# Attention's product with V: one fp32 operand in two column halves of the array in place of a split operand in whole-array matmuls

## The chip, the cores and the metric

The kernel runs on one core of a Trainium2 chip. A core has a matrix engine (TensorE, with a loader for its stationary operand), VectorE, ScalarE, GpSimd, and queues that issue DMAs. Each engine executes its own instructions in order and waits for the others through semaphores. The metric is the device time of one execution in microseconds; lower is better.

## What is computed

Two layers of a hybrid block run on 1024 latent tokens and 256 context tokens of width 1024. Each layer has a projection into four groups of heads (a state-space mixer, a gated recurrence, global attention, windowed attention), an output projection and an MLP. The change is in the attention of groups C (global) and D (windowed). Cut to that, the reference is:

```python
def block(qblk):                       # group C, 128 queries at a time
    s = einsum('bqhgd,bkhd->bhgqk', qblk, k_all) * scale
    pr = softmax(s, axis=-1)
    return einsum('bhgqk,bkhd->bqhgd', pr, v_all)

# group D: 128 queries see three blocks of 128 keys around them, the context, and a sink logit
pr = softmax(concatenate([s_band, s_ctx, s_sink], axis=-1), axis=-1)
o = (einsum('bnhgqk,bnkhd->bnqhgd', pr[..., :nk], vw)
     + einsum('bnhgqk,bkhd->bnqhgd', pr[..., nk:nk + n_ctx], vc))
```

There are four query heads of width 64 in each group and two key heads, so two query heads share a key head. Everything is fp32.

## The kernel before, in words

The kernel keeps fp32 accuracy with the faster matmul type fp32r by splitting operands: a high part rounded to fp32r and a low part, the remainder. `mm3` (lines 141 to 143) takes a product as three matmuls of such parts; most of the kernel's matmuls are these, in the projections.

Attention is done in units of one key head and its two query heads. `unit_proj` makes a unit's queries, keys and values for ten tiles of 128 tokens, and `unit_post` finishes two tiles at a time. It writes V as a tile of 128 columns per key block: columns 0 to 63 hold the fp32r high part (a ScalarE copy), columns 64 to 127 the low part (VectorE's subtraction, line 572).

`attention` walks over query tiles. For each, `attn_head` or `attn_both` makes the scores in PSUM, VectorE takes the maximum (L648), ScalarE the exponential. `attn_av` then multiplies the probabilities by V. Its `turn` takes two key blocks: TensorE transposes four 128x128 pieces (two blocks, two heads, L718) into one PSUM tile `pt`; ScalarE copies that tile as fp32r into `th` (recorded under its helper's line, L130); VectorE subtracts it from the original into the low part `tl` (L722). `prod`, run one turn later, adds two matmuls for each key block into the PSUM tile `po`: V's two parts times `th` (L727) and times `tl` (L728), each 128 columns stationary by 256 moving, fp32r. So po's partitions 0 to 63 hold the high part's product and 64 to 127 the low part's; at the end ScalarE copies the lower half (`lo`), VectorE adds the two (L744) and scales by the reciprocal sums (L746), which TensorE has spread out by two transposes (L741).

A global tile has ten key blocks, a windowed one five (four at the two ends of the sequence), a context tile two. Over both layers that makes 488 products of a query tile and a key block. Two `pt` tiles, three `qk` tiles and one `po` tile rotate in PSUM, and eight tiles tagged `s` in SBUF serve `th`, `tl` and others.

Attention is not run alone. `weave` interleaves its steps with those of another stage's projections, and the framework's scheduler puts the resulting instructions of each engine into one order, by its own costs. That order is fixed when the kernel is built, so a change of instructions also moves their neighbours. The modulation product (L319, in `mod_bank`) is the one place that already uses column tiles: fp32, 32 columns stationary, 512 moving, at four column positions.

Of the kernel before, what the change touches and what calls it, by code (L numbers as in the profile page):

```python
# [8 lines left out]
F32R = mybir.dt.float32r  # L9
# [4 lines left out]
P = 128  # L14
# [26 lines left out]
def f(ap):  # L41
    return ap.bitcast(F32)
# [51 lines left out]
class Net:  # L94
# [390 lines left out]
    def unit_proj(self, l, h, ws, rope_r, with_dt, need_ctx):  # L485

        nc = self.nc
        hh, hl = h
        nw = WU if with_dt else 256
        ws = [[t.rearrange("p (k c) -> p k c", k=4) for t in w] for w in ws]  # L490
        q = self.U()[:, :].rearrange("p (c d) -> p c d", d=P)
        kT = self.U(F32R)
        V = self.U(F32R).rearrange("p (c d) -> p c d", d=P)
        if with_dt:
            self.dtr = self.tp.tile([P, NT, 8], F32, tag="dtr", name="dtr", bufs=1)
        g = self.L[l]["rw"][:, rope_r:rope_r + 128]
        posts, half = [], None
        for tp in range(NT // 2):
            qkv = self.B()
            n1 = self.B()  # L500
            qkv3 = qkv.rearrange("p (a c) -> p a c", a=2)
            ps2 = self.PS() if not with_dt else None
            kv_only = tp == 0 and not with_dt and not need_ctx
            if kv_only:

                for k in range(KD):
                    wh, wl = (t[:, k % 4, P:256] for t in ws[k // 4])
                    self.mm3(ps2[:, 0:256], wh, wl, hh.at(k, 0, 256), hl.at(k, 0, 256), k == 0, k == KD - 1)
                    if k % 4 == 3:
                        yield 1.3  # L510
                self.copy_a(n1[:, 0:256], ps2[:, 0:256])
                for a in range(2):
                    nc.tensor.transpose(ps2[:, 256 + a * P:256 + a * P + P], n1[:, a * P:a * P + P], self.ident)
                last = self.copy_a(qkv3[:, :, P:256], ps2[:, 256:512].rearrange("p (a c) -> p a c", a=2))
            for a in range(0 if kv_only else 2):
                tt = 2 * tp + a
                t0 = tt * P
                if (0 if t0 < CTX else CTX + (t0 - CTX) // 512 * 512) not in hh.done:
                    yield from hh.pending
                ps = self.PS()[:, :nw] if with_dt else ps2[:, a * 256:a * 256 + 256]  # L520
                for k in range(KD):
                    wh, wl = ws[k // 4]
                    self.mm3(ps, hh.at(k, t0, P), hl.at(k, t0, P), wh[:, k % 4, :nw], wl[:, k % 4, :nw], k == 0, k == KD - 1)
                    if k % 4 == 3:
                        yield 1.3
                if with_dt:
                    last = self.copy_a(qkv3[:, a, :], ps[:, 0:256])
                    self.copy_a(self.dtr[:, tt, :], ps[:, 256:264])
            if not with_dt and not kv_only:
                last = self.copy_a(qkv, ps2)  # L530
            if half:
                with self.tc.issue_after(last.ins):
                    posts.append(half())
            if len(posts) == 2:
                posts.pop(0)()
                yield 0.3
            half = self.unit_post(tp, qkv3, n1[:, 0:384], q, kT, V, g, kv_only)
        self.tails = posts
        self.half = half
        return q, kT, V  # L540

# [8 lines left out]

    def unit_post(self, tp, qkv3, n1, q, kT, V, g, kv_only):
        nc = self.nc

        q0 = 2 if kv_only else 0
        nh = 3 - q0
        qk = qkv3[:, :, 64 * q0:192]
        v = qkv3[:, :, 192:256]
        vs = V[:, 2 * tp:2 * tp + 2, :]
        n1v = n1.rearrange("p (a c) -> p a c", a=2)
        n14 = n1.rearrange("p (a g d) -> p a g d", a=2, d=64)  # L560
        self.act(n1v[:, :, 64 * q0:192], qk, AF.Square)
        ss = self.tiny(2 * nh)
        ss3 = ss.rearrange("p (a g) -> p a g", a=2)
        nc.vector.tensor_reduce(ss3, n14[:, :, q0:3], axis=AX.X, op=ALU.add)

        if not kv_only:
            nc.vector.tensor_scalar(ss3[:, :, 0:2], ss3[:, :, 0:2], 64.0 * EPS, None, op0=ALU.add)
        nc.vector.tensor_scalar(ss3[:, :, nh - 1:nh], ss3[:, :, nh - 1:nh], 1.0 / 64.0, EPS, op0=ALU.mult, op1=ALU.add)
        rs = self.tiny(2 * nh)
        nc.gpsimd.tensor_tensor(rs, ss, self.mhalf.to_broadcast([P, 2 * nh]), op=ALU.pow)  # L570
        self.copy_a(vs[:, :, 0:64], v)
        nc.vector.tensor_sub(vs[:, :, 64:128], v, f(vs[:, :, 0:64]))
        def half():
            nc.vector.tensor_mul(n14[:, :, q0:3], qk.rearrange("p a (g d) -> p a g d", d=64),
                                 rs.rearrange("p (a g) -> p a g", a=2)[:, :, :, None].to_broadcast([P, 2, nh, 64]))
            qd = q[:, 2 * tp:2 * tp + 2, :]
            ks = n14[:, :, 2]
            gq = g[:, None, None, 0:64].to_broadcast([P, 2, 2, 64])
            gk = g[:, None, 64:128].to_broadcast([P, 2, 64])
            q4 = qd.rearrange("p a (g d) -> p a g d", g=2)  # L580
            nc.vector.tensor_mul(ks, ks, gk)
            if tp == 0 and not kv_only:
                nc.vector.tensor_mul(q4, n14[:, :, 0:2], gq)
            if tp:
                nc.vector.tensor_mul(n14[:, :, 0:2], n14[:, :, 0:2], gq)
                n3 = qkv3[:, :, 0:192]
                n1x, n3x = (t.rearrange("p a (g x h e) -> p a g x h e", g=3, x=2, h=2) for t in (n1v, n3))

                rc = slice(2 * tp - 2, 2 * tp), slice(8, 9)
                bc = [P, 2, 3, 16]  # L590
                for x in range(2):
                    for hf in range(2):
                        nc.vector.tensor_mul(n3x[:, :, :, x, hf], n1x[:, :, :, x, 1 - hf],
                                             self.sin[:, rc[x], None, hf].to_broadcast(bc))
                for x in range(2):
                    for hf in range(2):
                        nc.vector.tensor_mul(n1x[:, :, :, x, hf], n1x[:, :, :, x, hf],
                                             self.cos[:, rc[x], None].to_broadcast(bc))
                nc.vector.tensor_add(qd, n1v[:, :, 0:128], n3[:, :, 0:128])
                nc.vector.tensor_add(ks, ks, n3[:, :, 128:192])  # L600

            st = qkv3.rearrange("p a (s d) -> p a s d", d=64)[:, :, 0:2]
            self.copy_a(st[:, :, 0].bitcast(F32R), ks)
            nc.vector.tensor_sub(st[:, :, 1], ks, st[:, :, 0])

            def post():
                pt = self.PS("qk")
                for a in range(2):
                    nc.tensor.transpose(pt[:, a * P:a * P + P], st[:, a].rearrange("p s d -> p (s d)"), self.ident)
                self.copy_a(kT[:, 2 * tp * P:2 * tp * P + 256], pt[:, 0:256])  # L610
            return post
        return half
# [92 lines left out]

    def attn_av(self, prs, V, keys, mix):

        nc = self.nc
        kcs = [(k0 // P) + j for (k0, n) in keys for j in range(n // P)]
        po = self.PS("po")  # L710

        def turn(i):
            two = kcs[i:i + 2]
            w = 256 * len(two)
            pt = self.PS("pt")
            for e in range(len(two)):
                for hd in range(2):
                    nc.tensor.transpose(pt[:, e * 256 + hd * P:e * 256 + hd * P + P],  # L718
                                        prs[hd][0][:, (i + e) * P:(i + e) * P + P], self.ident)
            th, tl = self.S(w, F32R), self.S(w, F32R)  # L720
            self.copy_a(th, pt[:, :w])
            nc.vector.tensor_sub(tl, pt[:, :w], f(th))  # L722

            def prod():
                for e, kc in enumerate(two):
                    c = slice(e * 256, e * 256 + 256)
                    nc.tensor.matmul(po[:, :256], V[:, kc, :], th[:, c], start=i + e == 0, stop=False)  # L727
                    nc.tensor.matmul(po[:, :256], V[:, kc, :], tl[:, c], start=False, stop=i + e == len(kcs) - 1)  # L728
            return prod
        prod = None  # L730
        for i in range(0, len(kcs), 2):
# [901 lines left out]
```

## Time and profile before

| what | value |
|---|---|
| median of three runs | 3107.41 us (3104.35 to 3108.75) |
| profiled execution | 3102.39 us |
| its span, first to last instruction | 3100.6 us |
| TensorE busy | 2972.3 us, 96% |
| VectorE busy | 2195.9 us, 71% |
| ScalarE busy | 1516.4 us, 49% |
| GpSimd busy | 800.6 us, 26% |
| mean granted TensorE clock | 0.988 of full speed |

A busy time is the union of an engine's instructions. Matmuls are pipelined: a record runs on into its successors, so the step from one start to the next tells what a matmul costs in a stream, and the recorded duration does not. PE is TensorE, PEld its weight loader, DVE VectorE, ACT ScalarE, POOL GpSimd. L722 is line 722 of the kernel; the changed kernel's lines are shifted by one to two behind the edits.

### The profile page before, as it was taken

The numbers are of one execution on the slowest core, as the hardware profiler recorded it, in microseconds if no ns is written. First come the engines' busy times: TensorE is split into PE (matmuls) and PEld (weight loads), VectorE is DVE, ScalarE is ACT, GpSimd is POOL, SyncE is SP. The second block draws the span as 40 slices with busy tenths as digits, with TensorE's granted clock in tenths as the row PEclk, the third lists the DMA queues.
The fourth block names the chain that finished last, engine by engine and source line by source line (L and its number), as shares of the span: only waits on it lengthen the run. The fifth ranks groups of instructions, "written<-read, shape, count | busy, mean of one in ns | idle before, by whom it ended". The sixth has DMA issues, their size and how long they took to land.

```text
span 3100.6 us, 45540 instructions
## 1 busy us (share of the span) xinstructions
PE 2972.3 (96%) x16210; PEld 2458.7 (79%) x16210; DVE 2195.9 (71%) x4385; ACT 1516.4 (49%) x3570; POOL 800.6 (26%) x708
## 2 busy tenths in 40 slices
PE   5998998989999999999999999999899999999999
PEld 2788887788889887788888688887788778778887
DVE  5778777787742656577777777778787886667775
ACT  4675776676544444321112577676675544442120
POOL 2214123241454100222111512223342510032220
PEclk9999998999999999999999999999999999999999
DMA  8200012330355545642222400112422564553231
GB/s 283 64 18 25 20 37 72 98 138 33 125 168 157 177 152 182 218 146 85 77 84 78 147 18 18 28 40 70 140 82 71 171 205 138 166 179 104 87 104 62
DMA packets 241076, 330.71 MB, mean 107 GB/s; under 512 B 37328, under 2 KB 159824, under 8 KB 240848
## 3 DMA queue, kind: packets, MB, share of 16 engines
q1 hardware_dynamic: 213200, 281.64, 28.5%
q10 hardware_dynamic: 27648, 46.15, 4.0%
q8 instruction: 128, 2.10, 0.3%
q14 instruction: 100, 0.82, 0.1%
HBM read 253.28 MB, written 74.45 MB: 106 GB/s over the span
## 4 chain that ended last, share of the span: by engine, by line
PE 58%; DVE 5%; ACT 4%; DMA 2%; POOL 2%; issue 2%; ACTq 0%; SPq 0%; POOLq 0%; DVEq 0%
PE qk L143 8%; PE qk L142 8%; PE qk L141 8%; PE pm L143 6%; PE pm L141 6%; PE pm L142 6%; PE pt L142 3%; PE pt L143 3%; PE pt L141 3%; PE pt L718 1%; DVE u L136 1%; PE po L727 1%; POOL wl L246 1%; PE po L728 1%; DMA u<-in_w_ffn 1%
## 5 line engine op out<-in xcount | busy, mean ns | idle before, releaser
L246 POOL TENSOR_TENSOR wl<-raw,wh 128x512 fp32r<-128x512 f32 (+1 forms) x224 | 318.8, 1437 | 1215.9 <-ACT wh L130 916.5
L141 PE MATMUL pm<-u,wh 128*128 128x512 f32 (+1 forms) x1271 | 473.8, 373 | 4.1 <-DVE u L136 2.8
L143 PE MATMUL pm<-u,wl 128*128 128x512 f32 (+1 forms) x1271 | 467.5, 368 | 1.3 <-POOL wl L246 1.3
L142 PE MATMUL pm<-u,wh 128*128 128x512 f32 (+1 forms) x1271 | 466.5, 367 | 0.0
L130 ACT ACTIVATE wh<-raw 128x512 fp32r<-128x512 f32 (+1 forms) x224 | 135.6, 628 | 484.2 <-PE qk L142 159.8
L143 PE MATMUL qk<-u,wl 128*128 128x512 f32 (+1 forms) x874 | 326.7, 374 | 1.0 <-POOL wl L246 1.0
L141 PE MATMUL qk<-u,wh 128*128 128x512 f32 (+1 forms) x874 | 324.5, 372 | 1.9 <-DVE b L1342 1.0
L130 ACT ACTIVATE s<-pt 128x512 fp32r<-128x512 f32 (+4 forms) x548 | 251.2, 467 | 120.2 <-PE pt L718 74.4
L142 PE MATMUL qk<-u,wh 128*128 128x512 f32 (+1 forms) x810 | 300.2, 371 | 2.2 <-POOL u L409 1.8
L136 DVE SCALAR_TENSOR_TENSOR u<-pm,mods,u 128x512 f32<-128x512 f32 (+1 forms) x313 | 216.5, 693 | 90.4 <-PE pm L143 89.2
L141 PEld LDWEIGHTS pm<-u,wh 128*128 128x128 f32 x1271 | 243.1, 191 | 41.2 <-DVE u L136 4.4
L143 PEld LDWEIGHTS pm<-u,wl 128*128 128x128 f32 x1271 | 242.6, 191 | 35.4 <-POOL wl L246 2.7
L142 PEld LDWEIGHTS pm<-u,wh 128*128 128x128 f32 x1271 | 243.1, 191 | 30.8
L136 DVE SCALAR_TENSOR_TENSOR u<-qk,mods,u 128x512 f32<-128x512 f32 (+1 forms) x294 | 203.7, 693 | 84.2 <-PE qk L143 83.4
L133 ACT ACTIVATE b<-b 128x512 f32<-128x512 f32 (+4 forms) x256 | 146.1, 571 | 154.6 <-DVE b L1346 123.4
L133 ACT ACTIVATE e<-qk,t 128x512 f32<-128x512 f32 (+2 forms) x336 | 188.3, 571 | 42.3 <-DVE t L651 27.2
L722 DVE TENSOR_TENSOR s<-pt,s 128x512 fp32r<-128x512 f32 (+1 forms) x256 | 166.8, 661 | 39.7 <-ACT s L130 37.2
L1394 DVE TENSOR_TENSOR u<-e,u 128x256 fp32r<-128x256 f32 (+1 forms) x160 | 160.3, 1019 | 48.8 <-ACT u L130 27.6
L141 PEld LDWEIGHTS qk<-u,wh 128*128 128x128 f32 x874 | 165.2, 189 | 34.3 <-ACT u L130 1.7
L143 PEld LDWEIGHTS qk<-u,wl 128*128 128x128 f32 x874 | 164.6, 188 | 31.7 <-POOL wl L246 1.8
L141 PE MATMUL pm<-wh,u 128*128 128x256 f32 (+1 forms) x592 | 177.8, 301 | 3.3 <-ACT b L133 1.7
L142 PEld LDWEIGHTS qk<-u,wh 128*128 128x128 f32 x810 | 152.9, 189 | 31.3 <-POOL u L409 2.7
(325 smaller groups left out, 7526.3 us busy)
## 6 DMA issues: line engine op xcount, KB each, us to landing
raw<-in_w_ffn SPq DMA_DIRECT2D x184, 256.0 KB, 2.9
e<-in_w_mod SPq DMA_DIRECT2D x64, 512.0 KB, 4.5
u<-in_w_ffn SPq DMA_DIRECT2D x60, 512.0 KB, 5.1
m<-b ACTq DMA_DIRECT2D x96, 256.0 KB, 2.0
e<-m SPq DMA_DIRECT2D x32, 640.0 KB, 4.3
u<-in_w_mod SPq DMA_DIRECT2D x32, 512.0 KB, 6.3
e<-m SPq DMA_DIRECT2D x32, 512.0 KB, 3.9
raw<-in_w_in SPq DMA_DIRECT2D x48, 256.0 KB, 2.9
```

Of the source, the lines that this page charges most:

```text
L130: return self.nc.scalar.activation(o, i, AF.Copy, **k)
L133: self.nc.scalar.activation(o, i, fn, **k)
L136: self.nc.vector.scalar_tensor_tensor(o, a, s, b, op0=op0, op1=op1)
L141: mm(o, ah, bh, start=start, stop=False, skip_group_check=part)
L142: mm(o, ah, bl, start=False, stop=False, skip_group_check=part)
L143: mm(o, al, bh, start=False, stop=stop, skip_group_check=part)
L246: self.nc.gpsimd.tensor_sub(l, raw, f(h))
L718: nc.tensor.transpose(pt[:, e * 256 + hd * P:e * 256 + hd * P + P], prs[hd][0][:, (i + e) * P:(i + e) * P + P], self.ident)
L722: nc.vector.tensor_sub(tl, pt[:, :w], f(th))
L727: nc.tensor.matmul(po[:, :256], V[:, kc, :], th[:, c], start=i + e == 0, stop=False)
L728: nc.tensor.matmul(po[:, :256], V[:, kc, :], tl[:, c], start=False, stop=i + e == len(kcs) - 1)
L1394: self.nc.vector.tensor_sub(al[:, t], raw[:, t], f(ah[:, t]))
```

## The change

V is kept whole, as fp32, in columns 0 to 63 of its tile, and its low part is no longer made. The transposed probabilities leave PSUM in one copy, without a remainder; ScalarE makes that copy in even turns and VectorE in odd ones. The product takes one fp32 matmul for each key block, 64 columns stationary by 256 moving; the first block of a turn goes to the array's columns 0 to 63 and po's partitions 0 to 63, the second to columns and partitions 64 to 127. The two halves hold sums over different key blocks, and the addition of the halves at the end is what it was. A windowed tile with five blocks has a last turn with one block, in the first half alone.

```diff
-        V = self.U(F32R).rearrange("p (c d) -> p c d", d=P)
+        V = self.U().rearrange("p (c d) -> p c d", d=P)
...
         self.copy_a(vs[:, :, 0:64], v)
-        nc.vector.tensor_sub(vs[:, :, 64:128], v, f(vs[:, :, 0:64]))
...
-            th, tl = self.S(w, F32R), self.S(w, F32R)
-            self.copy_a(th, pt[:, :w])
-            nc.vector.tensor_sub(tl, pt[:, :w], f(th))
+            tp = self.S(w)
+            if i // 2 % 2:
+                nc.vector.tensor_copy(tp, pt[:, :w])
+            else:
+                self.copy_a(tp, pt[:, :w])
 
             def prod():
+
                 for e, kc in enumerate(two):
-                    c = slice(e * 256, e * 256 + 256)
-                    nc.tensor.matmul(po[:, :256], V[:, kc, :], th[:, c], start=i + e == 0, stop=False)
-                    nc.tensor.matmul(po[:, :256], V[:, kc, :], tl[:, c], start=False, stop=i + e == len(kcs) - 1)
+                    nc.tensor.matmul(po[64 * e:64 * e + 64, :256], V[:, kc, 0:64], tp[:, e * 256:e * 256 + 256],
+                                     start=i == 0, stop=i + e >= len(kcs) - 2, skip_group_check=True,
+                                     tile_position=(0, 64 * e))
```

The order on TensorE, in the seventh query tile of the first global unit, before. L718 are the transposes, L727 and L728 the products, L141 to L143 a woven projection, L645 scores of the next tile:

```order
L718 MATMUL pt<-rnd,e 128x128 x4
L727 MATMUL po<-s,u 128x256
L728 MATMUL po<-s,u 128x256
L727 MATMUL po<-s,u 128x256
L728 MATMUL po<-s,u 128x256
L718 MATMUL pt<-rnd,e 128x128
L141 MATMUL pm<-u,wh 128x512
L727 MATMUL po<-s,u 128x256
L142 MATMUL pm<-u,wh 128x512
L143 MATMUL pm<-u,wl 128x512
L645 MATMUL qk<-u,s 128x512
L728 MATMUL po<-s,u 128x256
```

The same tile after; the transposes are L717 there, the product L728, the scores L644:

```order
L717 MATMUL pt<-rnd,e 128x128 x4
L728 MATMUL po<-s,u 64x256 x2
L717 MATMUL pt<-rnd,e 128x128 x4
L143 MATMUL pm<-u,wl 128x512
L141 MATMUL pm<-u,wh 128x512
L142 MATMUL pm<-u,wh 128x512
L143 MATMUL pm<-u,wl 128x512
L644 MATMUL qk<-u,s 128x512
L728 MATMUL po<-s,u 64x256 x2
L717 MATMUL pt<-rnd,e 128x128 x4
L728 MATMUL po<-s,u 64x256 x2
```

Where four whole-array products stood, in a row or spread between others, two products in halves stand side by side, with whole-array matmuls before and behind them. In the whole program the 488 products stand as 215 such pairs, 24 single ones, 7 rows of four and 2 rows of three.

The order on VectorE, in the ninth tile of that unit, before. L648, L651 and L658 are the softmax's reductions:

```order
L722 TENSOR_TENSOR s<-pt,s 128x512
L651 TENSOR_REDUCE t<-t 128x1
L722 TENSOR_TENSOR s<-pt,s 128x512
L658 TENSOR_REDUCE t<-t 128x1
L659 RECIPROCAL t<-t 128x1
L648 TENSOR_REDUCE t<-qk 128x1
L722 TENSOR_TENSOR s<-pt,s 128x512 x2
L648 TENSOR_REDUCE t<-qk 128x1 x2
L136 SCALAR_TENSOR_TENSOR u<-b 128x512
L722 TENSOR_TENSOR s<-pt,s 128x512
```

And after, where the copy is L721 and the reductions are L647, L650 and L657:

```order
L647 TENSOR_REDUCE t<-qk 128x1 x2
L721 COPY s<-pt 128x512
L650 TENSOR_REDUCE t<-t 128x1
L721 COPY s<-pt 128x512
L657 TENSOR_REDUCE t<-t 128x1
L658 RECIPROCAL t<-t 128x1
L647 TENSOR_REDUCE t<-qk 128x1
L136 SCALAR_TENSOR_TENSOR u<-b 128x512
L647 TENSOR_REDUCE t<-qk 128x1
```

Five subtractions of this tile have gone, and two copies stand among the reductions.

## Rows read from the trace of the kernel before

**Rows 1.** The page, part 1: busy us (share of the span) xinstructions

```profile
PE 2972.3 (96%) x16210; PEld 2458.7 (79%) x16210; DVE 2195.9 (71%) x4385; ACT 1516.4 (49%) x3570; POOL 800.6 (26%) x708
```

**Rows 2.** Busy time by stretch: the attention stretches, two of six and their sum

```profile
core 0: us, PE busy (x) PEld busy (x) DVE busy (x) ACT busy (x) POOL busy (x), PEclk, DMA share, GB/s
100.00:250.00 150.00, 146.05 (x931) 125.18 (x930) 112.60 (x289) 104.03 (x273) 33.33 (x44) 1.00 0.11 26
...
610.00:800.00 190.00, 178.77 (x1134) 155.97 (x1134) 142.23 (x373) 122.29 (x377) 54.27 (x57) 0.98 0.23 83
...
sum 940.00, PE 909.06 PEld 774.66 DVE 707.68 ACT 646.18 POOL 231.06; mean PE 151.51 PEld 129.11 DVE 117.95 ACT 107.70 POOL 38.51
```

**Rows 3.** Groups by line and shape: busy us, mean ns | idle before, releasers

```profile
L727 PE MATMUL po<-s,u 128*128 128x256 f32 x488 | 153.5, 321 | 4.5 <-ACT s L130 2.6 <-DVE s L746 0.9
L728 PE MATMUL po<-s,u 128*128 128x256 f32 x488 | 132.2, 292 | 7.2 <-DVE s L722 6.8 <-DVE t L692 0.4
L722 DVE TENSOR_TENSOR s<-pt,s 128x512 fp32r<-128x512 f32 x232 | 156.7, 685 | 28.1 <-ACT s L130 25.6
L722 DVE TENSOR_TENSOR s<-pt,s 128x256 fp32r<-128x256 f32 x24 | 10.1, 421 | 11.6 <-ACT s L130 11.6
L572 DVE TENSOR_TENSOR u<-b,u 128x128 fp32r<-128x128 f32 x40 | 14.5, 361 | 1.7 <-ACT u L130 1.7
L648 DVE TENSOR_REDUCE t<-qk 128x1 f32<-128x512 f32 x128 | 85.1, 680 | 10.0 <-PE qk L646 9.3
L1216 DVE CAST u<-s 128x512 fp32r<-128x512 f32 x36 | 21.3, 598 | 0.1
L130 ACT ACTIVATE s<-pt 128x512 fp32r<-128x512 f32 x232 | 135.2, 597 | 72.5 <-PE pt L718 70.2 <-DVE t L651 1.4
```

**Rows 4.** Lines 727, then 728: matmul or loader idle before them until (us, times)

```profile
  ACT s L130: 27.5, 91
...
  DVE s L722: 20.0, 31
```

**Rows 5.** TensorE in order of time, four products in a stream: start us, us

```profile
752.58 0.28 PE L727 MATMUL po<-s,u 128*128 128x256 f32 x1
752.70 0.28 PE L728 MATMUL po<-s,u 128*128 128x256 f32 x1
752.82 0.28 PE L727 MATMUL po<-s,u 128*128 128x256 f32 x1
752.94 0.28 PE L728 MATMUL po<-s,u 128*128 128x256 f32 x1
```

**Rows 6.** The same view: two column tiles between whole-array matmuls of 264 columns

```profile
57.59 0.28 PE L142 MATMUL pm<-wl,u 128*128 128x264 f32 x1
57.71 0.29 PE L143 MATMUL pm<-wh,u 128*128 128x264 f32 x1
57.92 1.05 PE L319 MATMUL po<-e,csil 128*32 128x512 f32 x4
58.91 0.39 PE L143 MATMUL pm<-wh,u 128*128 128x264 f32 x1
```

**Rows 7.** The same view: two rounds of four column tiles

```profile
1284.55 0.40 PE L142 MATMUL qk<-u 128*128 128x512 f32 x1
1284.78 0.40 PE L143 MATMUL qk<-u 128*128 128x512 f32 x1
1285.11 1.92 PE L319 MATMUL po<-u,csil 128*32 128x512 f32 x16
1286.96 0.39 PE L141 MATMUL pt<-u,wh 128*128 128x256 f32 x1
1287.19 0.28 PE L142 MATMUL pt<-u,wh 128*128 128x256 f32 x1
1287.30 0.28 PE L143 MATMUL pt<-u,wl 128*128 128x256 f32 x1
```

**Rows 8.** Weight loads of lines 319 and 727: ns min/median/max

```profile
L319 PEld LDWEIGHTS po<-e,csil x256: 105/109/154, 55.0 to 2205.9; 128*32 128x32 f32 x128
L727 PEld LDWEIGHTS po<-s,u x488: 186/188/337, 123.2 to 2378.6; 128*128 128x128 f32 x163
```

## The prediction

> **What bounds the kernel now.** I read the page first, then the attention stretches by themselves, then single instructions. By the page TensorE is busy 96% of the span, VectorE 71%, ScalarE 49% [rows 1]. All 488 (query tile, key block) products that the change touches lie in six stretches, 940 us in all: there TensorE is busy 909 of 940 us, VectorE 708, ScalarE 646, at a granted clock of 0.98 to 1.00, the level of 2.4 GHz [rows 2]. So in these stretches TensorE sets the pace, and VectorE has a quarter of its time free. The reader should see that the two engines which the change relieves, VectorE and ScalarE, are not the ones that run out of time; they matter only where TensorE stands still for them. Two such places belong to the change: L727 found TensorE or its weight loader idle for ScalarE's copy for 27.5 us in 91 cases, L728 for VectorE's subtraction for 20.0 us in 31 cases [rows 4]; counted on TensorE's matmul part alone the idle time before the two lines is 4.5 and 7.2 us [rows 3].
>
> Busy times of matmuls overlap their successors, so I take a matmul's price from start to start. In a stream of whole-array matmuls the four of a pair of key blocks (L727, L728, L727, L728) start 0.12 us apart [rows 5].
>
> **VectorE and ScalarE.** Off VectorE go 256 subtractions L722 (156.7 + 10.1 us) and 40 of L572 (14.5 us): 181 us [rows 3]. Every second evacuation becomes a VectorE copy, 96 of 128x512 (two of five turns in each of 64 global tiles, one in each of 32 windowed ones). No copy of fp32 out of PSUM on VectorE stands in the trace; bounds are the 512-wide cast out of SBUF at 598 ns and the reduction out of PSUM at 680 ns [rows 3], and I take 0.65 us, 62 us in all. Net VectorE loses about 119 us, ScalarE 96 x 0.60 = 57 us [rows 3]. On the path this is worth nothing by itself; its worth is in waits, below. The copies that move queue on VectorE among the maxima of the scores (L648, L647 after), where a product already waited for L722 before, so no new wait arises there. A turn also takes one tile of the rotating eight instead of two; at worst that changes nothing.
>
> **TensorE, the term that decides.** Gone are 976 matmuls of 256 columns at 0.12 us, 117 us. In come 488 fp32 matmuls of 64 x 256 in column tiles. The trace has one like them: L319, fp32, 32 columns wide, 512 moving, four column tiles. It tells three things.
> First, the tiles do run at once: each fp32 matmul leaves two records, so the sixteen of 1285.11 to 1286.96 are eight matmuls, two rounds of four tiles, in 1.85 us [rows 7]; a single round, of two tiles, lasts from 57.92 to the next matmul at 58.91, 0.99 us [rows 6]. A round therefore streams for 0.86 us and carries 0.13 us of its own at its end.
> Second, a visit has a price at the door. The matmul ahead of L319 holds it up for 0.21 instead of 0.12 us (57.71 to 57.92 [rows 6]) and 0.33 instead of 0.23 (1284.78 to 1285.11 [rows 7]): 0.10 us, since the array empties first.
> Third, so does the way out: the first whole-array matmul behind it keeps its successor 0.23 instead of 0.12 us (1286.96 to 1287.19, then 1287.30 [rows 7]), because its weights could not be loaded beforehand: 0.11 us.
> For 256 columns the stream halves, 0.43 us. The weights are 64 wide: their load is between 0.11 us (32 wide) and 0.19 us (128 wide) [rows 8], by a straight line about 0.03 us over L319's. A visit of one pair: 0.43 + 0.13 + 0.10 + 0.11 + 0.03 = 0.80 us, against 4 x 0.12 = 0.48 before.
> From the order of the changed program: 215 visits of one pair, 24 of a lone matmul (the fifth block of a middle windowed tile, which has no partner and costs the same 0.80), 7 of two pairs and 2 of a pair and one (1.23 each). Sum: 172 + 19.2 + 8.6 + 2.5 = 202 us, so TensorE gets 202 - 117 = 85 us more to do. The bounds of a pair's price are 0.43 us (nothing paid but the stream) and 1.23 us (the halves one after the other). I take 0.80 since L319 is the same kind of visit, in the same kind of neighbourhood.
> On this the Trainium skill has two rules, in "TensorEngine Tiling (Array Packing)". Its table in the section "Theoretical Speedup" promises up to 2x for a dimension of at most 64; alone it would leave the stream's 0.43 us and the change a small gain (the first rival). Its section "Key Properties" says that changing the tiling mode drains the engine, which speaks against a mixed stream such as this; the 0.10 and 0.11 us of [rows 6, 7] agree with it.
>
> **What comes back.** The wait for L722 ends for good: 20.0 us [rows 4]. Of the 27.5 us for ScalarE's copy I take back 5: three in eight of those copies leave ScalarE, but the first product behind a transpose still needs its copy. Together 25 us, between bounds of 11.7 [rows 3] and 47.5 us [rows 4]. Of the other standstill of TensorE in these stretches (940 - 909 = 31 us [rows 2]) a later TensorE and a lighter VectorE absorb some; between 0 and 31 I take 15. Late next is TensorE itself, with the projections woven in between.
> Sum against the profiled execution of 3102.4 us (span 3100.6): 3102.4 + 85 - 25 - 15 = 3147 us. The median of the three runs shown is 5 us above that execution, so 3152 us.
>
> **The rivals.**
> *No price at the door, faster.* Two halves of 64 are not four quarters of 32, and it may be that the array goes over into halves without emptying, or that the loads hide. Then a visit costs its stream alone: 215 x 0.43 + 24 x 0.43 + 9 x 0.86 = 110 us against 117, so -7, and with the 25 us of waits 3071, by the median 3076 us. For it: only four-way tiles of 32 stand in the trace. Against it: the gaps are the same with two tiles in use [rows 6] as with four [rows 7]. It is the theoretical rule's case. Chance 0.17. It decides once a visit costs less than about 0.55 us: then the saved waits outweigh it.
> *The stalls take it all, no change.* If the order of instructions, which moves with the change, and the lighter VectorE remove every wait named, 47.5 + 31 = 78.5 us come back against 85: 3109, by the median 3114 us. For it: VectorE loses a sixth of its work in these stretches. Against it: it needs every wait to go, and TensorE is already 97% busy there [rows 2], so most of the added work finds no gap to fall into. Chance 0.13, of which 0.10 within 0.2% and 0.03 faster, if the order alone helps.
> *The halves take turns, much slower.* If two 64-wide fp32 tiles don't run at once, 231 pairs cost 0.43 us more, 99 us: 3251 us. Against it: [rows 7]. Chance 0.06.
>
> **How the numbers follow.** The forecast has 0.64, and its own range is 3120 (nearly all waits absorbed) to 3192 (none). About 0.2% (6 us) is what a measurement of this kernel can tell from no change. Faster: 0.17 + 0.03 = 0.20; same 0.10; slower 0.64 + 0.06 = 0.70. The range 3080 to 3195 holds the forecast, the no-change case and the upper part of the first rival; the third rival and the rest of the first, under 0.2 together, are left out.
>
> **What would show it.** In the changed kernel two L728 matmuls should start within some 10 ns of each other, the next whole-array matmul some 0.6 us after them, and its successor 0.23 instead of 0.12 us later; the matmul ahead should hold them up 0.10 us longer than its like. The waits for L722 should be gone, VectorE's busy time down by about 119 and ScalarE's by about 57 us, with no gain from it, and the six stretches together longer by about 45 us, everything else as before. If whole-array matmuls follow a pair after 0.43 us the first rival is right; if two tiles of a pair start 0.4 us apart, the third. If the visits cost what I say and the time still doesn't grow, I have underrated what VectorE holds up.

## The result, and the profile after

The changed kernel takes 3149.97 us (median of four runs, 3149.56 to 3150.48) against 3107.51 us before: 1.0138 times as long, 95% interval 1.0121 to 1.0156. The prediction was 3152 us, slower, with 3080 to 3195 as its range. The profiled execution spans 3148.6 us, 48 us more than before. The time came out where it was forecast; one of the steps by which the sum got there did not hold, and the experiments below are mostly about that one.

The page's first part, after: busy us (share of the span) xinstructions.

```profile
PE 3019.9 (96%) x16210; PEld 2384.5 (76%) x16210; DVE 2100.9 (67%) x4185; ACT 1473.3 (47%) x3474; POOL 792.1 (25%) x708
```

Against [rows 1], TensorE is busy 48 us longer, VectorE 95 and ScalarE 43 us less. The span grew by as much as TensorE's busy time; that two other engines were relieved did not shorten it. The number of TensorE's records is the same, since each of the 488 fp32 products leaves two where two fp32r products left one each.

The groups of the change, after: line, engine, operation, shapes, count, then busy us, mean ns of one, and idle before with its releasers.

```profile
L728 PE MATMUL po<-s,u 128*64 128x256 f32 x976 | 166.5, 405 | 7.0 <-ACT s L130 4.1 <-DVE s L748 1.2 <-DVE s L721 1.0
L130 ACT ACTIVATE s<-pt 128x512 f32<-128x512 f32 x136 | 81.2, 597 | 85.6 <-PE pt L717 84.9
L721 DVE COPY s<-pt 128x512 f32<-128x512 f32 x96 | 65.8, 686 | 47.8 <-PE pt L717 47.0
```

The copies are in the numbers that the prediction gave, 136 of the 232 wide ones of [rows 3] left on ScalarE and 96 on VectorE, each at 686 ns, as long as the subtraction of [rows 3] had been. Before these copies both engines sit idle for TensorE's transposes (L717), 85 and 47 us; ScalarE's copies did so before the change too, for 70 us [rows 3]. TensorE in its turn still waits for the copies, as shown further down.

TensorE in order of time, after, around one visit to the column tiles between whole-array matmuls of 256 columns: start us, us, engine, line.

```profile
681.21 0.28 PE L142 MATMUL pm<-u,wh 128*128 128x256 f32 x1
681.32 0.28 PE L143 MATMUL pm<-u,wl 128*128 128x256 f32 x1
681.53 0.65 PE L728 MATMUL po<-s,u 128*64 128x256 f32 x4
682.12 0.39 PE L141 MATMUL pm<-u,wh 128*128 128x256 f32 x1
682.34 0.28 PE L142 MATMUL pm<-u,wh 128*128 128x256 f32 x1
682.46 0.28 PE L143 MATMUL pm<-u,wl 128*128 128x256 f32 x1
```

This is the forecast's visit, piece by piece. The matmul ahead holds the pair up for 0.21 instead of 0.12 us (681.32 to 681.53), the pair itself lasts 0.59 (681.53 to 682.12), and the first matmul behind it takes 0.22 instead of 0.12 (682.12 to 682.34): 0.09 + 0.59 + 0.10 = 0.78 us, against 0.80 predicted from L319 and 0.48 before [rows 5]. Both halves run at once, the two first records 7 ns apart. The loader's records fit the last part: inside the stream the weights of L143 go in at 681.21, 0.11 us ahead of their matmul, those of the L141 behind the visit at 682.11, 0.01 us ahead. Not every visit is as dear. Behind 166 of the 248 a transpose of 128 columns comes next, and its step grows by 0.05 us only (0.164 instead of 0.109, medians), which makes 0.73 us.

The doors, as I call the way in and the way out, have a name in the view of waits: idle time that ended in nothing the profile shows, "issue". The largest five such rows of TensorE's weight loader, after: engine, what it was about to write, line, then idle us in all, times, longest us.

```profile
PEld pm L141 <- issue: 28.7, 51, 0.8
...
PEld po L728 <- issue: 24.9, 120, 0.4
...
PEld po L743 <- issue: 24.5, 63, 0.6
...
PEld pt L717 <- issue: 20.0, 52, 0.4
...
PEld pt L625 <- issue: 13.8, 36, 0.4
```

They sum to 112 us. L728 are the products; the other four are what stands behind a visit: projections (L141), transposes (L717 and L625) and L743, the transposes of the sums. In the kernel before the same view has 15.9 us for L141 and 1.9 for L727, and no row for the others among its 200 largest.

The products' own waits, after: line 728, idle before it until (us, times). Behind it, from the same view of line 644, the scores, what they waited for.

```profile
  ACT s L130: 33.6, 84
...
  ACT e L133: 17.2, 55
```

Before, the products waited 47.5 us for ScalarE and VectorE [rows 4]; now 33.6 us for ScalarE's copy, and 2.2 for VectorE's. But the scores, which had waited 5.5 us for ScalarE's exponential to free a PSUM tile, now wait 17.2. In this view the products wait 12 us less and the scores 12 us more.

### The profile page after: what moved, and what is told of

Read it like the earlier page. It is cut to its first block, busy times and chain, and to the rows that moved or that the text cites. A ratio compares the mean times of both kernels' runs of the same rounds, so it can differ in the third digit from the quotient of the medians.

```text
span 3148.6 us, 45096 instructions
## 1 busy us (share of the span) xinstructions
PE 3019.9 (96%) x16210; PEld 2384.5 (76%) x16210; DVE 2100.9 (67%) x4185; ACT 1473.3 (47%) x3474; POOL 792.1 (25%) x708
## 4 chain that ended last, share of the span: by engine, by line
PE 55%; DVE 6%; DMA 4%; issue 3%; ACT 3%; POOL 2%; SPq 0%; ACTq 0%; DVEq 0%; POOLq 0%
PE qk L143 7%; PE qk L142 7%; PE qk L141 7%; PE pm L141 6%; PE pm L143 6%; PE pm L142 6%; PE pt L142 3%; PE pt L141 3%; PE pt L143 3%; DMA u<-in_w_ffn 2%; PE po L728 2%; PE pt L717 1%; POOL wl L246 1%; ACT b L133 1%; DVE u L136 1%
## 5 line engine op out<-in xcount | busy, mean ns | idle before, releaser
L141 PE MATMUL pm<-u,wh 128*128 128x512 f32 (+1 forms) x1271 | 480.6, 378 | 3.6 <-DVE u L136 2.9
L143 PE MATMUL pm<-u,wl 128*128 128x512 f32 (+1 forms) x1271 | 468.1, 368 | 0.3 <-POOL wl L246 0.3
L141 PE MATMUL qk<-u,wh 128*128 128x512 f32 (+1 forms) x874 | 324.4, 372 | 4.5 <-DVE b L1344 2.8
L143 PE MATMUL qk<-u,wl 128*128 128x512 f32 (+1 forms) x874 | 326.4, 374 | 0.9 <-POOL wl L246 0.9
L141 PEld LDWEIGHTS pm<-u,wh 128*128 128x128 f32 x1271 | 243.6, 192 | 52.4 <-issue 11.6
L143 PEld LDWEIGHTS pm<-u,wl 128*128 128x128 f32 x1271 | 242.8, 191 | 40.5 <-issue 4.6
L130 ACT ACTIVATE s<-pt 64x256 fp32r<-64x256 f32 (+4 forms) x452 | 197.9, 439 | 148.9 <-PE pt L717 85.8
L141 PEld LDWEIGHTS qk<-u,wh 128*128 128x128 f32 x874 | 164.9, 189 | 37.1 <-DVE b L1344 3.6
L143 PEld LDWEIGHTS qk<-u,wl 128*128 128x128 f32 x874 | 164.6, 188 | 31.6 <-POOL wl L246 1.6
L141 PE MATMUL pm<-wh,u 128*128 128x256 f32 (+1 forms) x592 | 180.3, 305 | 3.3 <-ACT b L133 1.7
L142 PE MATMUL pm<-wl,u 128*128 128x256 f32 (+1 forms) x592 | 173.2, 293 | 6.2 <-POOL wl L246 6.2
```

The costliest lines, as they stand in the source:

```text
L130: return self.nc.scalar.activation(o, i, AF.Copy, **k)
L141: mm(o, ah, bh, start=start, stop=False, skip_group_check=part)
L142: mm(o, ah, bl, start=False, stop=False, skip_group_check=part)
L143: mm(o, al, bh, start=False, stop=stop, skip_group_check=part)
```

## The experiments

### VectorE's and ScalarE's side alone

TensorE keeps the products of before; only the evacuation is the changed kernel's.

```diff
-            th, tl = self.S(w, F32R), self.S(w, F32R)
-            self.copy_a(th, pt[:, :w])
-            nc.vector.tensor_sub(tl, pt[:, :w], f(th))
+            tp = self.S(w, F32R)
+            if i // 2 % 2:
+                nc.vector.tensor_copy(tp, pt[:, :w])
+            else:
+                self.copy_a(tp, pt[:, :w])
...
-                    nc.tensor.matmul(po[:, :256], V[:, kc, :], th[:, c], start=i + e == 0, stop=False)
-                    nc.tensor.matmul(po[:, :256], V[:, kc, :], tl[:, c], start=False, stop=i + e == len(kcs) - 1)
+                    nc.tensor.matmul(po[:, :256], V[:, kc, :], tp[:, c], start=i + e == 0, stop=False)
+                    nc.tensor.matmul(po[:, :256], V[:, kc, :], tp[:, c], start=False, stop=i + e == len(kcs) - 1)
```

> VectorE's and ScalarE's side of the change alone: the probabilities leave PSUM in one copy (even turns ScalarE, odd turns VectorE) and no subtraction is made, while TensorE keeps the 976 whole-array fp32r products of 256 columns of the kernel before. Left out: the low parts of V and of the probabilities; the high part's product is counted twice. Theory (TensorE's visits to the column tiles are the loss, the lighter VectorE and ScalarE give back about 40 us of waits): 3067 to 3085 us. Rival 1 (the lighter engines are off the path and give nothing, or the new order costs): 3100 to 3115 us. Rival 2 (VectorE was what held the attention stretches up, all 78 us of waits go): about 3030 us.

Measured: 3117.35 us, 1.0042 times the kernel before (1.0027 to 1.0057). Neither my theory nor the second rival: the lighter engines gave nothing back, and the kernel is some 12 us slower, 2 us above the first rival's range. This kernel also had 40 small fills on GpSimd in place of V's subtraction, so it was run again without them.

> e2_relief once more without its 40 fills on GpSimd, V's low part again by VectorE's subtraction as in the kernel before; of VectorE's work only the 256 subtractions L722 are gone, with 96 copies taken over (105 us net). Left out: the low part of the probabilities, the high part's product is counted twice. If the fills hid a gain in e2_relief: 3070 to 3095 us. If the lighter VectorE and ScalarE give nothing by themselves: 3105 to 3120 us.

Measured: 3113.35 us, 1.0027 (1.0016 to 1.0037). The fills were not the reason. Where did the 20.0 us go that L728 had waited for the subtraction [rows 4]? Three lines of e10_relief_sub: the first product of a turn (L730 there), idle before it; the second product's loader (L731), with its idle time behind the second bar; and the scores (L645), idle before them.

```profile
  ACT s L130: 41.3, 99
...
L731 PEld LDWEIGHTS po<-s,u 128*128 128x128 f32 x488 | 92.6, 190 | 0.9
...
  ACT e L133: 17.4, 59
```

The second product indeed no longer waits: 0.9 us of idle time are left. But the first one now waits 41.3 us for ScalarE's copy where it had waited 27.5 [rows 4], and the scores wait 17.4 us for ScalarE's exponential to free a PSUM tile, where the kernel before has this line for its scores:

```profile
  ACT e L133: 5.5, 16
```

That is 13.8 + 11.9 = 26 us of new waits for 20 us that ended. The wait was not removed, it moved one place up the chain. My reading is that TensorE arrives earlier at the next link when one gets shorter. (The profiled executions lie further apart than the medians, 17 us against 7, so the two rows are a picture of where the time went and not its exact size.) There is a second effect. Measured from the first to the last transpose of each of the six stretches, attention takes 756 us before and 753 us here, but the rest of the program grows from 2345 to 2365 us. TensorE's work other than products, taken at its steps in a stream, is 585 us inside the stretches before and some 574 here: some 10 us of it has only moved out, by the new order, and the rest is waits. Every kernel here with the one-piece copy and the interleaving as it was has 2352 to 2372 us outside, the two that keep a second VectorE pass (the next one and e8_double) 2342 to 2343.

### TensorE's side alone

```diff
-            tp = self.S(w)
-            if i // 2 % 2:
-                nc.vector.tensor_copy(tp, pt[:, :w])
-            else:
-                self.copy_a(tp, pt[:, :w])
+            th, tp = self.S(w), self.S(w)
+            self.copy_a(th, pt[:, :w])
+            nc.vector.tensor_add(tp, pt[:, :w], th)
```

This is against the changed kernel; V's low part is also made again.

> TensorE's side of the change alone: the 488 fp32 products of 64 x 256 in two column halves, while VectorE still makes a second tile from PSUM in each turn (256 of them, an addition in place of the subtraction) and V's low part, as before, and ScalarE copies in every turn. Left out: the right probabilities, the product is taken with twice their value; V's low part is made and not used. Theory: 85 us more on TensorE, of which some 10 to 15 fall into gaps: 3107 + 70 to 85 = 3177 to 3192 us, above the changed kernel by what the other side gives back. Rival 1 (the other side gives nothing): 3145 to 3155 us, as the changed kernel. Rival 3 (the loss comes from the evacuation and its order, not from the column tiles): 3110 to 3125 us.

Measured: 3150.61 us, 1.0143 (1.0128 to 1.0158), the same as the changed kernel. The first rival holds: the whole loss is TensorE's product, and the relief of the other engines adds nothing to it and takes nothing from it. The busy times show that the relief really is absent here, VectorE at the 2195.9 us of [rows 1]:

```profile
PE 3023.3 (96%) x16210; PEld 2385.1 (76%) x16210; DVE 2195.9 (70%) x4385; ACT 1521.5 (48%) x3570; POOL 796.1 (25%) x708
```

and its products, line 727 there, wait no longer than the changed kernel's, though they wait for VectorE's second pass and not for a copy:

```profile
  DVE s L722: 33.4, 64
  issue: 30.1, 127
```

33.4 us here, 33.6 in the changed kernel, 47.5 before. The scores, though, do not wait longer here than before, where it was 5.5 us in 16 cases:

```profile
  ACT e L133: 3.5, 13
```

So the longer wait of the scores comes with the relief, 17.4 us in e10_relief_sub and 17.2 in the changed kernel, and not with the products.

The steps of TensorE's records tell the same for all four kernels. I took every matmul that is not a product at what its shape takes in a stream of the kernel before (2673 us in all, in each kernel), the products and their doors at their undisturbed steps, and put what is left down as a wait of the instruction that came late; some 20 us lie outside TensorE's first and last record. Below I call this the account of the steps; the table has us.

| kernel | products with doors | waits, all | before products | before scores |
|---|---|---|---|---|
| before | 116 | 291 | 25 | 15 |
| e10_relief_sub | 116 | 309 | 34 | 24 |
| e3_product | 190 | 264 | 12 | 12 |
| after | 188 | 268 | 13 | 19 |

(These waits are time that matmuls lost; the view of waits counts the loader's idle time, part of which passes while matmuls still run.) Without the relief the column tiles take TensorE 74 us more and its waits shrink by 27 us; with the relief it is 72 and 41. The relief itself shortens the waits in neither pair, 291 to 309 us and 264 to 268.

### More for VectorE

```diff
             nc.vector.tensor_sub(tl, pt[:, :w], f(th))
+            nc.vector.tensor_sub(tl, pt[:, :w], f(th))
```

> The kernel before with each of the 256 subtractions L722 made twice into the same tile, 167 us more for VectorE in the attention stretches and 0.68 us more between a transpose and the product with the low part; all else as before. In e2_relief taking 119 us off VectorE gave nothing. Theory now (VectorE's load in these stretches is off the path, TensorE has other work while it waits): 3105 to 3125 us. Rival (VectorE holds the stretches up, and e2_relief hid its gain behind a changed order): 3107 + 60 to 120 = 3170 to 3230 us.

Measured: 3177.01 us, 1.0227 (1.0211 to 1.0243). The rival's range, and against my revised theory: the second subtractions take 164 us by their groups (L723), VectorE's busy time grows by 130 us, and the kernel takes 69 us more, about 0.4 to 0.5 us for each. The product with the low part (L729 there), idle before it, where [rows 4] had 20.0 us in 31 cases:

```profile
  DVE s L723: 42.6, 50
```

and that product as a group, with its idle time on the matmul part, where [rows 3] had 7.2 us:

```profile
L729 PE MATMUL po<-s,u 128*128 128x256 f32 x488 | 138.2, 303 | 16.6 <-DVE s L723 16.0
```

So more work for VectorE is felt, where less of it was not. "Off the path" was the wrong word for it. That the three engines' chains through a turn are about equally long, so that lengthening any of them is felt and shortening one leaves the others, is my reading; no run shows it for ScalarE. Nor does this run tell what about the second subtraction costs the time. It is load on VectorE and a later product at once, the order shifted (some 36 us of TensorE's other work moved into the stretches), and TensorE ran at the lower clock level, 1.2 GHz, for 118 us of the span instead of 72. Of its busy time 102 us fell there instead of 63, so up to 19 us of the 69 may be the clock, by my estimate (half of the 39 us more).

### Fewer visits

The products of several turns are held back and issued in a row, the last turn's first, so that all are ready when the first one is. The part that differs from the changed kernel, for two turns; for all of a tile, 2 is replaced by a number above five:

```diff
-            nxt = turn(i)
+            todo.append(turn(i))
...
-            if prod:
-                prod()
-                yield 0.43
-            prod = nxt
-        prod()
...
+            if len(todo) > 2 and i + 2 < len(kcs):
+                visit(todo[:2], False)
+                todo = todo[2:]
...
+        visit(todo, True)
```

> The changed kernel with the products of two or three turns put into one visit: the products wait until two (at a tile's end up to three) turns have been copied out and are then issued in a row, the last turn first. 105 visits to the column tiles in place of 248, the same 488 products, copies and sums. Theory (about 0.35 us for each entry and exit, 0.43 us for each pair): 143 x 0.35 = 50 us less than the changed kernel, about 3100 us. Rival (the loss is the four passes of fp32 themselves, the entry costs little): within 10 us of 3150. Rival (products wait longer for their copies): above 3150 us.

Measured: 3118.28 us, 1.0041 (1.0026 to 1.0056) times the kernel before.

> The changed kernel with all products of a query tile in one visit behind its last copy: 73 visits in place of 248, the same products, copies and sums. Theory: 175 x 0.35 = 61 us less than the changed kernel, about 3089 us, or up to 15 us more where TensorE now waits at a tile's end for the last copy. Rival (four passes are the loss): within 10 us of 3150. Rival (products wait longer for their copies, the tile's end gets late): above 3150 us.

Measured: 3114.11 us, 1.0026 (1.0016 to 1.0035). Both rivals fall: with the same products, copies and sums the loss shrinks from 42 to 13 and 8 us when the visits go from 248 to 105 and 73. The entry and exit are the bulk of the loss. The full 50 and 61 us did not come, 32 and 36 did. The loader's "issue" time goes with the visits too: over all lines it is 154 us with 248 of them, 97 with 105 and 81 with 73, against 38 in the kernel before. One visit in e5_all, TensorE in order of time:

```profile
158.93 0.40 PE L143 MATMUL pm<-u,wl 128*128 128x512 f32 x1
159.26 2.38 PE L727 MATMUL po<-s,u 128*64 128x256 f32 x20
161.57 0.43 PE L751 MATMUL po<-rnd,t 128*128 128x128 f32 x2
```

Five pairs in 2.31 us (159.26 to 161.57): with 0.59 us for the first, four more at 0.43, to the hundredth what the working gave. By the account of the steps, products and doors take 133 us in e5_all, 55 less than in the changed kernel, close to the 61 expected; the waits grow by 18 us, to 286. Of these 18, 14 stand before the transposes (L717). They now come in a row of twenty and run into their two PSUM tiles. Idle before them in e5_all, for ScalarE's and VectorE's copies:

```profile
  ACT s L130: 25.3, 49
  DVE s L721: 5.2, 14
```

against 3.7 and 1.5 us in the changed kernel.

Since ScalarE's copies were waited for, VectorE took more of them, three of five turns and then all (the cut is of the second):

```diff
-            if i // 2 % 2:
-                nc.vector.tensor_copy(tp, pt[:, :w])
-            else:
-                self.copy_a(tp, pt[:, :w])
+            nc.vector.tensor_copy(tp, pt[:, :w])
```

> All products of a query tile in one visit, as in e5_all, with VectorE copying out the even turns (three of five) and ScalarE the odd ones. In e5_all TensorE's transposes and loads waited 25.3 us for ScalarE's copies and 5.2 for VectorE's. Theory (ScalarE's copies stand behind its exponentials, VectorE has time): 5 to 12 us less than e5_all, 3102 to 3109 us, no better than the kernel before. Rival (VectorE's copies stand behind its maxima as long): 3114 us or more.

Measured: 3109.18 us, 1.0006 (0.9997 to 1.0016).

> All products of a query tile in one visit, with VectorE alone copying out all turns; VectorE then has 256 copies in place of the 256 subtractions of the kernel before, ScalarE loses 256 copies. Theory (TensorE's waits for ScalarE's copies go, VectorE is as busy as before): 3095 to 3110 us. Rival (one engine for all copies makes the transposes wait for their two PSUM tiles): above 3114 us.

Measured: 3106.13 us, 0.9996 (0.9985 to 1.0008), as the kernel before. The busy times of e7_dve, and what its transposes (L717) waited for:

```profile
PE 2972.1 (96%) x16210; PEld 2406.2 (77%) x16210; DVE 2189.0 (70%) x4345; ACT 1393.7 (45%) x3314; POOL 803.7 (26%) x708
...
  DVE s L720: 11.4, 19
...
  ACT s L130: 1.2, 4
```

The transposes now wait for VectorE's copies, and 12.6 us in place of 30.5: the idle time moves with the engine that has the copies. VectorE has its old load, ScalarE 1393.7 instead of 1516.4 us [rows 1], and still nothing is won on the kernel before. By the account of the steps the products with their doors take 133 us here against 116 there, even in 72 visits; they hardly wait any more, 2 us against 25, but other matmuls wait 16 us longer, the transposes, scores and others. The next expectation has 21 us saved and 28 come back; put down to the instruction that came late, it is 7 and 16.

### The interleaving

The last try was whether the weights by which attention is woven with projections, set for the kernel before, give that gain back.

```diff
-DL = (0.12, 0.1, 0.04, 68, 55, 26, 28, 14, 28, 11, 15, 16, 12)
+DL = (0.12, 0.1, 0.04, 61, 49, 26, 28, 14, 28, 11, 15, 16, 12)
```

> e7_dve with the attention streams' weights in the interleaving cut by a tenth (68 to 61 and 55 to 49), so that more of the woven projections is issued ahead of each attention step. In e7_dve the products cost TensorE 21 us less than in the kernel before and 28 us came back as waits elsewhere. If the interleaving, tuned for the kernel before, is what gives the gain back, one of this and e12_faster is 8 to 20 us below e7_dve's 3106; if the waits are chains between the engines, both are at 3100 to 3125 us.

Measured: 3126.98 us, 1.007 (1.0055 to 1.0086).

> e7_dve with the attention streams' weights in the interleaving raised by a tenth (68 to 75 and 55 to 61), so that attention steps are issued earlier against the woven projections. Expected as for e11_slower: one of the two 8 to 20 us below 3106 if the interleaving is the cause, both at 3100 to 3125 us if not.

Measured: 3111.16 us, 1.0013 (1.0005 to 1.0022). Neither gains, so a tenth either way of these two weights is not the cause. e11_slower is even 2 us above the range expected of chains. Other weights were not tried.

### The same fp32 products over the whole array

The edit is against the changed kernel.

```diff
-                    nc.tensor.matmul(po[64 * e:64 * e + 64, :256], V[:, kc, 0:64], tp[:, e * 256:e * 256 + 256],
-                                     start=i == 0, stop=i + e >= len(kcs) - 2, skip_group_check=True,
-                                     tile_position=(0, 64 * e))
+                    nc.tensor.matmul(po[:, :256], V[:, kc, :], tp[:, e * 256:e * 256 + 256],
+                                     start=i + e == 0, stop=i + e == len(kcs) - 1)
```

> The changed kernel without column tiles: V's tile is filled with zeros in columns 64 to 127 and each of the 488 products is one fp32 matmul over the whole array, 128 x 256. Theory: 488 x 0.43 us of stream with no entry and exit, 210 us, against 215 x 0.77 + 24 x 0.76 + 9 x 1.2 = 195 us as the changed kernel's trace shows its visits: 10 to 20 us above the changed kernel, 3160 to 3170 us. Rival (the entry and exit cost little in the stream of other work, the overlap of the halves is what counts): 99 us of overlap are lost, about 3240 us. Rival (the loss is not TensorE's): 3150 us.

Measured: 3210.59 us, 1.0329 (1.0311 to 1.0347): between my theory and the rival. Again there were fills on GpSimd, and again they were taken away:

> e1_whole once more without its 40 fills on GpSimd: columns 64 to 127 of V's tile are written by the subtraction of the kernel before on VectorE (v minus its own copy, zeros). e1_whole took 3210 us where its products, by its own trace, hold TensorE only some 20 us longer than the visits of the changed kernel. If the fills on GpSimd were the rest: 3160 to 3175 us. If not (whole-array products leave TensorE's neighbours later, the waits are spread): 3195 to 3215 us.

Measured: 3209.6 us, 1.0328 (1.0309 to 1.0347). TensorE in order of time in e9_whole_sub, two products of two records each:

```profile
140.99 0.60 PE L718 MATMUL pt<-rnd,e 128*128 128x128 f32 x4
141.42 1.03 PE L729 MATMUL po<-s,u 128*128 128x256 f32 x4
142.29 0.60 PE L718 MATMUL pt<-rnd,e 128*128 128x128 f32 x4
```

0.87 us for the pair (141.42 to 142.29), 0.43 each, with no door on either side: 210 us in all, as expected. The "issue" rows are back to those of the kernel before, 17.2 us for the projections and 2.1 for the products:

```profile
PEld pm L141 <- issue: 17.2, 20, 1.3
...
PEld po L729 <- issue: 2.1, 1, 2.1
```

So that idle time belongs to the column tiles and not to fp32. The products' 210 us are 93 us above the 117 of the kernel before, and this kernel is 103 us slower: here no part of the added time was absorbed. Against the changed kernel the products are 23 us dearer by their steps (211 to 188) and the time 60 us longer. In part I can see it. The products wait longer for ScalarE's copies, and the projections for VectorE's evictions:

```profile
  ACT s L130: 41.9, 104
...
PEld pm L141 <- DVE u L136: 10.9, 4, 4.0
```

against 33.6 and 4.9 us in the changed kernel, 14 us more. By the account of the steps the waits are 303 us against 268, and 19 of these 35 stand before the products, 32 us against 13. So a longer visit does not by itself let the copies catch up: here a pair takes longer than in the column tiles, and its products wait more. One reading is that a wait which falls into the emptying of the array costs little more. The steps speak for it in part. The loader waited for another engine ahead of 99 of the changed kernel's visits and of 73 of e9_whole_sub's rows of products, 0.33 us in the median of both. In the changed kernel the matmul ahead of these 99 held them up for 0.10 us, that ahead of the visits without such a wait for 0.09; here it is 0.13 us with a wait and nothing without. Beyond the price of the door the waits cost 11 of 35 us there and 19 of 30 us here. That is some 11 us by an estimate (at 19 of 30 the 35 us would have cost 22); why the rest of TensorE waits less beside the column tiles stays open.

## Why the prediction was right, point by point

**The price of a visit.** Right, in each part: 0.09 + 0.59 + 0.10 = 0.78 us measured, 0.80 predicted from L319 [rows 6, 7]. All 248 visits come to some 188 us by the undisturbed steps of the records, 202 predicted, since two in three of them leave by the cheaper way; the added work of TensorE is 72 us, 85 predicted. (The expectation of e1_whole has 195 us, with the dearer way out for all.) That a visit of two halves of 64 behaves like one of quarters of 32 was the first rival's doubt, and it is settled: the array empties all the same. The rule of two column tiles for one at up to 2x in the Trainium skill ("TensorEngine Tiling (Array Packing)", section "Theoretical Speedup") holds for the stream, 0.43 us for two products where e9_whole_sub takes 0.87; most of it is lost again at the doors, 0.34 us in the visit shown. The section "Key Properties" of that page has the rule that a change of mode drains the engine, and no price.

**What comes back.** The forecast was 40 us; 24 came back (72 - 48), and the reason given was wrong. I put 25 us down to the products, by the end of the wait for L722 and a lighter ScalarE, and the 15 in part to a lighter VectorE. By the account of the steps the waits before products fell by 13 us, those before projections by 7 and before the rest by 7, and the scores waited 4 us longer. e3_product has no relief and the same time; e2_relief and e10_relief_sub have all of the relief and lose 7 to 12 us. What fails is the step "the wait for L722 ends for good: 20.0 us": the wait ended, and its time came back at the copy before it and at the scores, in e10_relief_sub 13.8 and 11.9 us, in the changed kernel 6.1 and 11.7. The waits that did get shorter got so beside the column tiles, and not by the relief; the reason stays open in the main. The step got its number from the right rows and its cause from a guess that a wait removed is time won. TensorE's work came out 13 us under the forecast and what came back 16 us under it. The two errors nearly cancel, so that the time lies 2 us from the forecast is in part luck.

**VectorE and ScalarE.** The copy was taken at 0.65 us and measured 0.686. VectorE lost 95 us, not 119, and ScalarE 43, not 57, with part of the difference left unexplained (by VectorE's groups it is 181 us off [rows 3] and 66 on, 115). Worth on the path: nothing, as said, and less than nothing with the order's shift. The text says that the 96 copies are two in each of 64 global tiles; there are 32 such tiles, with 64 copies, and the total of 96 is right.

**The rivals.** No price at the door: refuted by the visit above. The stalls take it all: refuted by the time, which is 42 us longer; that more work for VectorE costs time (e8_double) does not make less of it a gain. The halves take turns: refuted, 7 ns apart.

**Where the time would show.** I expected the stretches to carry all of the 45 us. From the first to the last transpose they are 32 us longer, and the rest of the program is 16 us longer, of which some 11 to 13 us is TensorE's work that the new order moved out of the stretches. The place was wrong by that, the amount not.

## What to carry to other kernels

Count a column-tiled matmul by visits, not by matmuls: two half-width fp32 products at once cost 0.43 us of stream and 0.34 us for going in and out. Against the same two products in fp32 over the whole array, 0.87 us, one pair already costs less, and the kernel with those was 60 us slower than the changed one. Against the split operand at 0.48 us a pair it would take some seven pairs in a row by an estimate (0.34 / 0.05); the rows of five here did not get there, and no kernel with them beat the one before. Before you credit a change with the wait it ends, name the next thing that the same engine will then wait for, and run the relief alone: in this kernel more work for TensorE or VectorE cost time, and less for VectorE and ScalarE gained none. A prediction can have the right sum with a wrong cause in it, and only experiments with one half of the change at a time tell.

## What the runs showed of the hardware

An fp32 product of 256 columns takes 0.43 us over the whole array, as two records of 0.22 us, and two 64-column products in the two halves take the same 0.43 us together. A row of five such pairs keeps that rate. A VectorE copy of 128x512 fp32 out of PSUM took 686 ns, the ScalarE copy 597 ns. What I had not expected: the idle time at the doors is booked as "issue" in the view of waits, 112 us over five lines in the changed kernel where the kernel before has 18 and the whole-array fp32 kernel 19. It shrinks with the number of visits, so beside column-tiled matmuls a large "issue" of the loader was a sign of mode changes here. And a wait removed can come back at the next instruction: with the relief the products stopped waiting 20 us for VectorE, and the scores waited some 12 us longer for ScalarE, with either kind of product.
